# Down projection of a ConvFFN layer: eight block products against seven, with the contraction in three parts

## The chip, the core and the metric

The kernel runs on one core of a Trainium2 chip. The core has a matrix engine (TensorE, PE in the profile, with PEld for its weight loads), a vector engine (VectorE, DVE), an engine for activations (ScalarE, ACT), a general one (GpSimd, POOL) and SyncE (SP), whose queue issues most of the transfers between HBM and the on-chip memory SBUF. Matmul results land in PSUM, in banks of 512 float32 per partition. The metric is the device time of one execution in microseconds, the median of several runs; a profiled execution adds a trace of every instruction.

## The reference

One layer of an encoder, for 1024 prompt frames and 32 sample frames (T = 1056 columns together). After the mixing branches the layer computes

```
hf = RMSNorm(x)
[a | u] = hf @ W_up                     W_up (1024, 5632)
a = causal depthwise conv3(a) + b_conv
x = x + RMSNorm((gelu(a) * u) @ W_down) W_down (2816, 1024)
y = x + (p @ W_ple) * sigmoid(x @ W_ple_gate)
```

All is float32. To keep that precision, a matmul takes each operand as a high part and a low remainder in the type `fp32r`, and sums three products: high x high, high x low, low x high. Making the two parts of an operand costs a cast on ScalarE and a subtraction on VectorE (a "split").

## The kernel before

Activations lie with channels on the 128 partitions and tokens along the columns. The stages of interest are the last three.

**Up projection** (from about 1162 us on). 22 units, one for each 128-channel tile of `a` and `u` (`up_unit`). A unit already works in seven products of block sums (the scheme of Strassen and Winograd): rows are split into two halves of the contraction, columns into `a` and `u`, tokens into quarters of H = 264, two quarters making a token half (a pass `p`). A product takes 4 contraction tiles x 2 token halves x 3 matmuls of 264 columns. The operands' seven block sums lie split in SBUF pages (`ops`, placed by `where`), and the weights' seven parts are made for each unit by `unit_parts`: GpSimd adds blocks, ScalarE casts, VectorE subtracts, into a ring `wb` of eight slots. `prepare` keeps three parts ahead. Three PSUM tiles X, Y and Z (two banks each) take the products: X the first and third, Y the second, fourth and sixth, Z the fifth and seventh, so a tile is used again two products later, once VectorE or ScalarE (`after`) has read it. `ff_tail` applies convolution, gelu and the product with `u`, one unit late, and stores the tile into `act_d` in HBM.

**Down projection** (from 1617 to 1872 us). Three token groups of M3 = 352; in each, two halves of four output tiles; for each, 22 contraction tiles, accumulated in four PSUM banks without interruption. The activations of a group come from HBM in four chunks (`load_chunk`), split by ScalarE and VectorE (L2111, L2112). The weights are loaded and split anew for each group (`next_w`, L182, L184). `d_out` copies a bank out and sums squares. While groups 1 and 2 run, `x2_part` does for the group before what follows the sum of squares: scale by the row factor and the gain, add `x1`, split (L2173, L2174, L227).

**Final gate** (from 1872 us). For two halves of four output tiles and three groups, a block of 24 matmuls of 352 columns (`block`), then tanh, two vector operations (`y_out`, L2216 to L2218), and one block later the transposes into rows and the stores (`y_done`, L2230 to L2252).

What sets the order: each engine runs its own queue in order. That order isn't the text's; a scheduler builds it, taking the instruction that comes first in the text among those whose inputs it expects to be ready, and `behind(...)` puts a block behind the latest instruction traced on the named engines. Buffers of a pool are handed on when their last reader is done, and a transfer issued on SP's queue that waits holds those behind it.

## Time and profile before

| | |
|---|---|
| three runs, median | 1982.42 us (1981.69 to 1982.99) |
| profiled execution, first to last instruction | 1980.2 us |
| the rest of an execution, median less span | 2.2 us |
| TensorE busy | 1963.0 us of the span, 14239 matmuls |
| VectorE busy | 1388.1 us |
| ScalarE busy | 1003.0 us |
| GpSimd busy | 259.2 us |
| HBM read, written | 177.89 MB, 65.32 MB |

The trace has no figure of its own for what lies around the span, so the third row is the difference to the median of the runs. A row of a group reads: line, engine, operation, output and inputs, shapes, count, then busy us in all and mean ns of one, then idle time of that engine before them and what ended it. Durations of matmuls and of vector operations overlap those of their neighbours a little; starts don't.

### The profile page before, as it was taken

The numbers are of one execution on the slowest core, as the hardware profiler recorded it, in microseconds if no ns is written. First come the engines' busy times: TensorE is split into PE (matmuls) and PEld (weight loads), VectorE is DVE, ScalarE is ACT, GpSimd is POOL, SyncE is SP. The second block draws the span as 40 slices with busy tenths as digits, with TensorE's granted clock in tenths as the row PEclk, the third lists the DMA queues.
The fourth block names the chain that finished last, engine by engine and source line by source line (L and its number), as shares of the span: only waits on it lengthen the run. The fifth ranks groups of instructions, "written<-read, shape, count | busy, mean of one in ns | idle before, by whom it ended". The sixth has DMA issues, their size and how long they took to land.

```text
span 1980.2 us, 37208 instructions
## 1 busy us (share of the span) xinstructions
PE 1963.0 (99%) x14239; PEld 1948.0 (98%) x14239; DVE 1388.1 (70%) x3059; ACT 1003.0 (51%) x2188; POOL 259.2 (13%) x391
## 2 busy tenths in 40 slices
PE   8999999999999999999999999999999999999998
PEld 8999999999999999999999999999999999999998
DVE  6777776888878888553555878877777784655552
ACT  7667777666656666451225663333333344444332
POOL 2111110000000000012001133333343300000000
PEclk9999999999999999999999999999999999999999
DMA  8533431311122211486558662222222245665542
GB/s 265 151 98 103 129 112 59 129 51 55 57 77 58 58 56 58 128 256 212 179 168 277 215 222 87 76 87 66 91 71 79 84 165 186 214 198 170 161 134 79
DMA packets 255256, 253.57 MB, mean 128 GB/s; under 512 B 14133, under 2 KB 221992, under 8 KB 255077
## 3 DMA queue, kind: packets, MB, share of 16 engines
q1 hardware_dynamic: 244917, 218.43, 35.4%
q0 software_dynamic: 10080, 32.73, 5.4%
q8 instruction: 112, 1.84, 0.4%
q14 instruction: 67, 0.55, 0.1%
q10 hardware_dynamic: 80, 0.03, 0.0%
HBM read 177.89 MB, written 65.32 MB: 123 GB/s over the span
## 4 chain that ended last, share of the span: by engine, by line
PE 76%; issue 12%; DVE 5%; DMA 3%; ACT 2%; POOL 1%; SPq 0%; POOLq 0%; DVEq 0%; ACTq 0%
PE mm L203 9%; PE mm L205 9%; PE mm L204 9%; PE st L2014 7%; PE st L2012 7%; PE st L2013 7%; PE G L1114 2%; PE Y L1111 2%; PE G L1113 2%; PE Y L1114 2%; PE Y L1113 2%; PE G L1111 2%; PE Z L1111 1%; PE Z L1113 1%; PE Z L1114 1%
## 5 line engine op out<-in xcount | busy, mean ns | idle before, releaser
L2012 PE MATMUL st<-op,wt 128*128 128x264 f32 x1232 | 348.8, 283 | 2.8 <-ACT Sp L2023 1.4
L2014 PE MATMUL st<-op,wt 128*128 128x264 f32 x1232 | 349.7, 284 | 0.0
L2013 PE MATMUL st<-op,wt 128*128 128x264 f32 x1232 | 347.7, 282 | 0.0
L2012 PEld LDWEIGHTS st<-op,wt 128*128 128x128 f32 x1232 | 231.2, 188 | 4.5 <-ACT Sp L2023 2.0
L2013 PEld LDWEIGHTS st<-op,wt 128*128 128x128 f32 x1232 | 231.4, 188 | 0.0
L2014 PEld LDWEIGHTS st<-op,wt 128*128 128x128 f32 x1232 | 230.8, 187 | 0.0
L182 ACT CAST wh<-wr 128x1024 fp32r<-128x1024 f32 x125 | 131.2, 1049 | 187.7 <-PE mm L204 138.7
L184 DVE TENSOR_TENSOR wl<-wr,wh 128x1024 fp32r<-128x1024 f32 x114 | 139.6, 1225 | 111.5 <-ACT wh L182 99.6
L203 PE MATMUL mm<-ac,wh 128*128 128x352 f32 x528 | 170.6, 323 | 0.0
L1756 ACT CAST wt<-wu 128x512 fp32r<-128x512 f32 x126 | 77.7, 619 | 183.2 <-POOL ab L1998 82.2
L205 PE MATMUL mm<-ac,wl 128*128 128x352 f32 x528 | 169.7, 321 | 0.0
L204 PE MATMUL mm<-ac,wh 128*128 128x352 f32 x528 | 169.4, 321 | 0.0
L203 PE MATMUL mm<-La,wh 128*128 128x384 f32 (+1 forms) x480 | 158.2, 330 | 0.0
L204 PE MATMUL mm<-Lb,wh 128*128 128x384 f32 (+1 forms) x480 | 155.4, 324 | 0.5 <-DVE Lb L773 0.4
L205 PE MATMUL mm<-La,wl 128*128 128x384 f32 (+1 forms) x480 | 154.9, 323 | 0.1
L203 PE MATMUL mm<-Ra,wh 128*128 128x264 f32 x512 | 145.4, 284 | 0.0
L204 PE MATMUL mm<-Rb,wh 128*128 128x264 f32 x512 | 145.0, 283 | 0.0
L205 PE MATMUL mm<-Ra,wl 128*128 128x264 f32 x512 | 145.0, 283 | 0.0
L1757 DVE TENSOR_TENSOR wt<-wu,wt 128x512 fp32r<-128x512 f32 x126 | 101.1, 804 | 47.0 <-ACT wt L1756 47.0
L205 PEld LDWEIGHTS mm<-ac,wl 128*128 128x128 f32 x528 | 99.4, 188 | 0.0
L204 PEld LDWEIGHTS mm<-ac,wh 128*128 128x128 f32 x528 | 99.2, 188 | 0.0
L203 PEld LDWEIGHTS mm<-ac,wh 128*128 128x128 f32 x528 | 99.1, 188 | 0.0
(553 smaller groups left out, 5756.1 us busy)
## 6 DMA issues: line engine op xcount, KB each, us to landing
wr<-in_w_down_dram SPq DMA_DIRECT2D x66, 512.0 KB
wu<-in_w_up_dram SPq DMA_DIRECT2D x42, 512.0 KB
wu<-in_w_in_dram SPq DMA_DIRECT2D x36, 512.0 KB
ac<-act_d SPq DMA_DIRECT2D x66, 176.0 KB
act_d<-Up SPq DMA_DIRECT2D x21, 528.0 KB
wr<-in_w_in_dram SPq DMA_DIRECT2D x21, 512.0 KB
wr<-in_w_out_dram SPq DMA_DIRECT2D x16, 512.0 KB
wl<-wr POOLq DMA_DIRECT2D x11, 512.0 KB, 4.9
```

The source lines that it names most:

```text
L182: S.copy(hi[:], raw[:])
L184: V.tensor_tensor(lo[:], raw[:], hi[:].bitcast(F32), op=ALU.subtract)
L203: E.matmul(ps, wh, a, start=first and n == 0, stop=False)
L204: E.matmul(ps, wh, b, start=False, stop=False)
L205: E.matmul(ps, wl, a, start=False, stop=last and n == len(ks) - 1)
L1111: E.matmul(o, wh, x[0][k], start=first and k == 0, stop=False, skip_group_check=True)
L1113: E.matmul(o, wh, x[1][k], start=False, stop=False, skip_group_check=True)
L1114: E.matmul(o, wl, x[0][k], start=False, stop=k == 3, skip_group_check=True)
L1757: V.tensor_tensor(t[:, 1], src, t[:, 0].bitcast(F32), op=ALU.subtract)
L2012: E.matmul(o, wh, xh, start=first and k == 0, stop=False, skip_group_check=True)
L2013: E.matmul(o, wh, xl, start=False, stop=False, skip_group_check=True)
L2014: E.matmul(o, wl, xh, start=False, stop=k == 3, skip_group_check=True)
```

## The change

The down projection becomes twelve more units of the scheme that the up projection has. The contraction of 22 tiles is taken as 11 pairs; the even and the odd tile of a pair are the two rows of the block scheme, two neighbouring output tiles its two columns (four pairs `cp_` in all), and the token quarters its columns on the other side. The 11 pairs are taken in three parts of 3, 4 and 4 (`KP`), since the operand pages hold four: part by part all four column pairs run, and each unit adds its result to accumulators in SBUF (`acc_t`, and `S_` for a shared sum). In the third part the sums are completed, and the squares are summed on the way.

The operands of the products: `act_sums` makes four block sums of each pair of activation tiles on VectorE beside every second up unit and stores them (`s_d`); three operands are plain blocks of the stored activations (`a_d`, in place of `act_d`). At the last up unit, and at the last unit of parts 0 and 1, each operand page is loaded anew as its last product ends (`load_op`, on SP's queue) and split in the steps that `SPLIT_AT` names. Weights of the down units are read as 128-column tiles and go through `unit_parts`; the raw weights of every second down unit lie in the ring `wb`.

The last down unit runs its seven products for one token half and then for the other. The normalisation of the first half's tokens is placed into the second. The gate goes by token quarters of 264: quarters 0 and 1 for the first four output tiles, in steps of two contraction tiles interleaved with `x2_pair`, then the rest. The block sums change the rounding of the result, within float32; nothing of the computation is left out.

```diff
-    act_d = [dp.tile([P, T], F32, name=f"act_d{f}") for f in range(NF)]
+    a_d = dp.tile([P, NF, T], F32, name="a_d")
+    s_d = {o: dp.tile([P, NF // 2, 2, H], F32, name=f"s_d{o}") for o in (1, 3, 4, 5)}
...
+    KP = ((0, 3), (3, 4), (7, 4))
+    DU = [(pt, cp_) for pt in range(3) for cp_ in range(4)]
+    NU = NF + len(DU)
...
+            tag, bufs = ("wr", 2) if u % 2 else ("wb", 8)
+            pt, cp_ = DU[u - NF]
+            j0, n = KP[pt]
+            for c in (2 * cp_, 2 * cp_ + 1):
+                t.append(wp.tile([P, KT, P], F32, tag=tag, name=nm("wd"), bufs=bufs))
+                dma(t[-1][:, :2 * n], rows_cols(w_down, 2 * j0 * P, c * P, P, 2 * n)[0])
...
+    def act_sums(j):
+        (b11, b12), (b21, b22) = act_blocks(2 * j), act_blocks(2 * j + 1)
...
+        V.tensor_tensor(d, b11, b12, op=ALU.subtract)
+        V.tensor_tensor(e, b12, b22, op=ALU.subtract)
+        dma(s_d[4][:, j], d)
+        dma(s_d[3][:, j], e)
+        yield
+        V.tensor_tensor(d, d, b22, op=ALU.add)
+        V.tensor_tensor(e, b21, d, op=ALU.subtract)
+        dma(s_d[1][:, j], d)
+        dma(s_d[5][:, j], e)
+        yield
+
+    def load_op(pt, p, i):
...
+        dma(t[:, 1, :n].bitcast(F32), src)
+
+    def split_op(pt, p, i):
+        n = KP[pt][1]
+        hi, lo = (ops[p][i][:, a, :n] for a in range(2))
+        S.copy(hi, lo.bitcast(F32))
+        V.tensor_tensor(lo, lo.bitcast(F32), hi.bitcast(F32), op=ALU.subtract)
+
+    SPLIT_AT = {3: 0, 4: 1, 6: 2, 7: 3, 9: 4, 10: 5, 11: 6}
...
                 mults(i, t, first, ps)
+                if u == NF - 1:
+                    for p in range(2):
+                        load_op(0, p, i)
+                    split_step(0, n)
...
+                if u and u % 2 == 0 and n in (2, 5):
+                    if n == 2:
+                        sums_of.append(act_sums(u // 2 - 1))
+                    with behind(V):
+                        next(sums_of[-1])
...
+    def down_unit(u):
...
+                for k in range(ng):
+                    wh, wl = w[:, 0, k, :], w[:, 1, k, :]
+                    xh, xl = ops[p][i][:, 0, k, :], ops[p][i][:, 1, k, :]
+                    E.matmul(o, wh, xh, start=first and k == 0, stop=False, skip_group_check=True)
+                    E.matmul(o, wh, xl, start=False, stop=False, skip_group_check=True)
+                    E.matmul(o, wl, xh, start=False, stop=k == ng - 1, skip_group_check=True)
...
+        for ps in ((0,), (1,)) if split_p else ((0, 1),):
+            for n, (i, t, first) in enumerate(steps):
+                if ps[0] == 0:
+                    prepare(7 * u + n + AHEAD)
+                mults(i, t, first, ps)
+                if cp_ == 3 and not last:
+                    for p in range(2):
+                        load_op(pt + 1, p, i)
+                    split_step(pt + 1, n)
+                if cp_ == 0:
+                    split_step(pt, 7 + n)
+                after(i, ps)
+                if split_p:
+                    beside_last(ps[0], n)
...
+    def x2_pair(q, cp_):
...
+        for a in range(2):
+            k = 2 * cp_ + a
+            V.scalar_tensor_tensor(ak[:, a], ak[:, a], g_pffn[:, k:k + 1], rb2[tp_][:, h], op0=ALU.mult,
+                                   op1=ALU.mult)
+        V.tensor_tensor(ak, ak, x1s[n], op=ALU.add)
+        z_ = slice(2 * cp_, 2 * cp_ + 2)
+        S.copy(xh[q][:, z_], ak)
+        V.tensor_tensor(xl[q][:, z_], ak, xh[q][:, z_].bitcast(F32), op=ALU.subtract)
...
+    def beside_last(p, n):
...
+        if n == 1:
+            with behind(E):
+                x2_norm(0)
...
+        elif n == 4:
+            with behind(E):
+                x2_rows(0)
+            x2_pair(0, 0)
+            gate_parts(3)
+        elif n == 5:
+            x2_pair(0, 1)
...
+    for kp in gate_two(0):
+        if kp < 2:
+            x2_pair(0, kp + 2)
+        if kp == 1:
+            with behind(E):
+                x2_norm(1)
+        if kp == 2:
+            x2_pair(1, 0)
+        if kp == 3:
+            with behind(E):
+                x2_rows(1)
+            x2_pair(1, 1)
+    gate_parts(4)
+    gate_parts(5)
+    for kp in gate_two(1):
+        if kp < 2:
+            x2_pair(1, kp + 2)
+        if kp == 2:
+            gate_parts(6, where[1][2])
+            gate_parts(7, where[1][3])
...
+    for m, (q, cp_) in enumerate(((0, 2), (1, 2), (0, 3), (1, 3))):
+        gate_one(q, cp_)
+        for kp in range(2):
+            x2_pair(2 + m // 2, 2 * (m % 2) + kp)
+    for cp_ in range(4):
+        for q in (2, 3):
+            gate_one(q, cp_)
+    late_y(0)
```

More of the change, by code (lines that the diff above doesn't have):

```diff
@@ L2268, in layer_kernel, with ep_q, acc_of @@
-    for l in late:
-        y_done(*l)
+    ep = ctx.enter_context(right("ep"))
+    nrm = ep.tile([P, 4, 8], F32, name="nrm")
+    def ep_q(name):
+        return ep.tile([P, 2, H], F32, tag="q", name=nm(name), bufs=4)
+    sqd = [ep_q("sqd") for _ in range(2)]
+    acc_t = [ep.tile([P, 4, 2, H], F32, name=f"acc{i}") for i in range(3)]
+    acc_t = [acc_t[1], acc_t[2], acc_t[0]]
+    S_ = page(lq, 3, [P, 4, 2, H], "S").bitcast(F32)
+    def acc_of(cp_):
+        if cp_ == len(acc_t):
+            acc_t.append(page(lq, 2, [P, 4, 2, H], "acc3").bitcast(F32))
+        return acc_t[cp_]
```

437 lines of the change are left out of this document (268 added, 169 removed).

## The prediction

> **What bounds the kernel now.** First the page of the profile: its span, the share of each engine, the slices, the chain that ended last.
>
> ```profile
> span 1980.2 us, 37208 instructions
> PE 1963.0 (99%) x14239; PEld 1948.0 (98%) x14239; DVE 1388.1 (70%) x3059; ACT 1003.0 (51%) x2188; POOL 259.2 (13%) x391
> ...
> PE   8999999999999999999999999999999999999998
> PEclk9999999999999999999999999999999999999999
> ...
> PE 76%; issue 12%; DVE 5%; DMA 3%; ACT 2%; POOL 1%; SPq 0%; POOLq 0%; DVEq 0%; ACTq 0%
> ```
>
> TensorE is busy 99% of the span at a full granted clock, and no slice after the first falls under 0.9 until the end. So a matmul taken away is time gained, and an idle stretch of TensorE is time lost, whichever engine caused it. Next the windows by stage (columns: busy us of PE, PEld, DVE, ACT, POOL with counts, granted clock, DMA share, GB/s) and the instructions that read `ac`, the operand of the old down projection.
>
> ```profile
> 1200.00:1597.00 397.00, 396.52 (x3273) 396.26 (x3272) 307.07 (x470) 136.58 (x196) 135.94 (x97) 1.00 0.25 79
> 1300.00:1400.00 100.00, 100.00 (x828) 100.00 (x827) 76.77 (x120) 34.91 (x50) 34.23 (x26) 1.00 0.26 81
> 1616.86:1872.05 255.19, 255.19 (x1612) 255.13 (x1610) 144.16 (x200) 112.86 (x156) 0.00 (x0) 1.00 0.56 186
> ...
> L203 PE MATMUL mm<-ac,wh x528: 320/322/408, 1617.0 to 1871.6; 128*128 128x352 f32 x176
> L205 PE MATMUL mm<-ac,wl x528: 317/322/325, 1617.3 to 1871.9; 128*128 128x352 f32 x176
> ```
>
> A matmul's shown duration (322 ns) overlaps the next one's, so I use starts. The down stage starts 3 x 528 = 1584 matmuls of 352 columns in 1872.05 - 1617.0 = 255.1 us: 161.0 ns each. The up stage, already in block sums, starts 828 of 264 columns in 100 us: 120.8 ns. 161.0 x 264/352 = 120.8, so cost goes by columns, with no fixed part per matmul in sight. VectorE is 77% busy in the up stage (307.07/397) and 56% in the down stage.
>
> **The change, part by part.**
>
> *Products.* 3 token thirds x 8 output tiles x 22 contraction tiles x 3 matmuls = 1584 of 352 become 4 column pairs x 11 contraction groups x 7 products x 2 token halves x 3 = 1848 of 264. 1848 x 0.1208 = 223.2 us against 255.1: **-31.9 us**. The gate keeps its columns: 576 x 352 = 768 x 264. I go by the two rates above, which are in the ratio of the columns. The Trainium skill speaks against that ("TensorE: Matmul & The Clock Gate", section "Wait — 56ns, not 53.3ns?"): a warm matmul costs N/2.4 ns and a fixed 2.5 ns or so, which narrower ones pay oftener. An estimate from that page is 236.3 - 207.9 = 28.4 us saved, 3.5 less, with which the sum below would end at 1973.
>
> *What the rest costs is stall of TensorE.* VectorE prices follow; its instructions overlap their neighbours, so I take start to start.
>
> ```profile
> 1606.37 1.23 DVE L1957 TENSOR_TENSOR Up<-a,Up 128x1024 f32<-128x1024 f32 x1
> 1607.52 0.18 DVE L1958 TENSOR_TENSOR Up<-a,Up 128x32 f32<-128x32 f32 x1
> 1607.62 0.70 DVE L2027 TENSOR_TENSOR ab<-st,rbT 128x528 f32<-128x528 f32 x1
> 1608.24 0.88 DVE L2112 TENSOR_TENSOR ac<-ac,ac 128x704 fp32r<-128x704 f32 x1
> ...
> 1122.59 2.43 DVE L1686 TENSOR_TENSOR op<-z,op 128x1056 fp32r<-128x1056 f32 x2
> 1128.50 0.43 DVE L1660 TENSOR_TENSOR sq<-x 128x264 f32<-128x264 f32 x1
> 1128.85 0.43 DVE L1662 TENSOR_TENSOR x<-x 128x264 f32<-128x264 f32 x1
> 1886.46 1.07 DVE L2173 SCALAR_TENSOR_TENSOR acc<-acc,gvec,rb 128x352 f32<-128x352 f32 x2
> ...
> L1757 DVE TENSOR_TENSOR wt<-sa,wt 128x512 fp32r<-128x512 f32 x20 | 13.6, 680 | 0.0
> L1949 DVE SCALAR_TENSOR_TENSOR a<-ab,cvec,a 128x1058 f32<-128x1058 f32 x19 | 30.8, 1623 | 22.8 <-ACT a L1945 22.8
> L1953 DVE SCALAR_TENSOR_TENSOR a<-ab,cvec,a 128x1058 f32<-128x1058 f32 x20 | 26.3, 1316 | 0.0
> ```
>
> So 1056 columns cost 2.43 - 1.26 = 1.17 us, 1024 1.15, 528 0.62, 264 0.35; by the slope, 792 (three groups, token half) 0.90, 512 0.60, 384 0.46. The two-scalar form costs 1.24 at 1058 and 0.49 at 352, so 0.41 at 264.
>
> *Block sums beside the up stage.* `act_sums` puts four 528-column operations into every second unit of 168 x 0.1208 = 20.3 us: 4 x 0.62 = 2.5 us, VectorE from 77% to 89% there. Its four stores and the DMA share of 0.25 leave room; the sum rewritten at step 5 waits for a store issued at step 2, 8.7 us earlier. Each PSUM tile is used again two products later, so VectorE may be late by one product (2.9 us). Cost 0; 0 to 2.
>
> *Into the first down unit.* A unit of contraction part 0 lasts 126 x 0.1208 = 15.2 us. VectorE has in it the tail of channel tile 21 (two two-scalar operations 2.5, products 1.25, leftovers of `done` 1.5), its block sums 2.5, the splits of operands 3 to 6 for both token halves 8 x 0.90 = 7.2, seven weight parts 7 x 0.46 = 3.2, two reads of PSUM 1.2: 19.2 us, 4.0 more than it has. The old kernel had the same tail there, and splits too (L2112), but ahead of their need. The splits are needed by the very next products, and VectorE takes its queue in order. **+4**; below, 0, if the three weight parts made ahead cover it; above, 8, if the waits inside the tail (ScalarE's gelu, the store before a sum is rewritten) aren't filled.
>
> *From part to part.* At the last column pair of a part each of the 14 operand pages is loaded again as its product ends and split in steps 3 to 11: 14 x 1.17 = 16.4 us more on VectorE over two units. With weight parts and PSUM reads at the same prices (13.4 and 18.9 us) that makes 29.8 of 35.5 us from part 0 to 1, 35.3 of 40.6 from 1 to 2: it fits in sum, but a step with a split has 0.60 + 2.34 + 0.62 = 3.56 us of work in 2.9, lateness grows to about 3 us, and one step is what the banks allow. The loads: 14 x 541 KB = 7.6 MB, and 1.05 MB of weights before them on SP's queue. Each load waits there for its product's end, and behind the seventh stand the weights of the next unit but one, whose first part is due 11.6 us later: with those late, the casts on ScalarE and all behind them are late.
>
> ```profile
> 855.00:860.00 5.00, 5.00 (x44) 5.00 (x43) 3.78 (x10) 3.52 (x9) 0.54 (x1) 1.00 0.94 282
> 860.00:865.00 5.00, 5.00 (x44) 5.00 (x43) 3.57 (x11) 3.13 (x8) 0.05 (x1) 1.00 0.95 285
> 1606.00:1610.00 4.00, 4.00 (x36) 4.00 (x35) 3.90 (x7) 3.40 (x6) 0.00 (x0) 1.00 1.04 370
> ```
>
> The first two rows are bursts of 264-column loads (runs of 1056 bytes, as here), the third of 352-column ones. At 283 GB/s 8.6 MB take 30.5 us. From part 0 to 1 there are 28 us between the end of the first product and the split of the last operand; from 1 to 2, 32; into part 0, 28 for 6.5 MB (23 us). So about 2 us short at one place, partly covered. **+1.5** for both; 0 to 6. GpSimd's weight sums go on as in the up stage (135.94 us in 397, 34%), with room for the ten additions of squares that part 2 gives it: 0.
>
> *The start of the gate.* Every output channel is complete only in the last unit, so the normalisation, which the old kernel did beside the down stage for two thirds of the tokens, now stands wholly ahead of the gate. The last unit runs one token half after the other (7 x 12 x 0.1208 = 10.1 us each). Count from the second half: the broadcast of the row factors is queued behind its fifth product, 7.25 us, plus the transposing matmuls and ScalarE's copy: 8.0. Then a pair of channel tiles of a token quarter (`x2_pair`) costs VectorE 2 x 0.41 + 2 x 0.62 = 2.06 us, with a ScalarE cast inside that the next pair can fill. Until quarters 0 and 1 are through: eight pairs 16.5, products 5 and 6 with their squares 4 x 0.35 = 1.4, the low parts of gate weights 3, 4, 5 at 1.15 = 3.4, the second normalisation 1.5, the first two outputs 4 x 0.63 = 2.5: 25.3 us. The last step of the gate's first half then ends at 8.0 + 25.3 + 1.45 = 34.8, where TensorE alone would be at 10.1 + 96 x 0.1208 = 21.7: 13.1 us. If outputs and weights 4 and 5 (4.8 us) come after the pairs it is 8.3. **+11**; 6, if half of the pairs' work finds earlier gaps, to 16, if each pair also waits out its cast. After that 8 pairs (16.5 us) stand beside 192 matmuls (23.2 us) and are covered.
>
> *Small work and the end.*
>
> ```profile
> 1876.84 0.22 DVE L1561 TENSOR_SCALAR nv<-tr 128x2 f32<-128x2 f32 x2 [2.01 <-PE tr L1558]
> 1879.73 0.16 DVE L220 SCALAR_TENSOR_TENSOR nr<-rst,nr 128x3 f32<-128x3 f32 x1
> ...
> 1960.86 0.49 PE L2230 MATMUL tr<-ident,y 128*128 128x128 f32 x3
> 1965.06 0.49 PE L2230 MATMUL tr<-ident,y 128*128 128x128 f32 x3
> ...
> 1973.25 0.32 PE L205 MATMUL mm<-x2r,wl 128*128 128x352 f32 x1
> 1977.09 0.33 SPq L2246 DMA_DIRECT2D out_dram<-yr  x1
> 1968.70:1980.20 11.50, 5.95 (x38) 5.30 (x36) 2.67 (x9) 2.42 (x10) 0.00 (x0) 0.91 0.23 63
> ```
>
> The first two rows are one normalisation's small operations: 3.05 us with two others between. From one group of three transposes to the next is 4.20 us, 24 matmuls (3.86) and 0.34: 0.113 a transpose. There are 80 instead of 72, and 18 more column sums and broadcasts, most of them where TensorE waits anyway: **+1.5** (1 to 3). After the last matmul the old kernel needs 1980.2 - 1973.4 = 6.8 us. The new one has two output groups left there, five PSUM copies and three or four stores more on queues that took 0.3 and 0.5 us each: **+1.2** (0 to 3).
>
> *Sum:* -31.9 + 4 + 1.5 + 11 + 1.5 + 1.2 = -12.7. The profiled span becomes 1980.2 - 12.7 = 1967.5. The median of the runs, 1982.42, lies 2.2 us above that span; I put the same around the new one: **1969.7 us**.
>
> **The rivals.**
>
> 1. *The stalls are mostly filled.* VectorE was free 44% of the old down stage (144.16 of 255.19 busy), ScalarE 56%, and the scheduler lets work that is ready pass work that isn't. With 0, 0, 6, 1.5 and 1.0: -23.4, 1959. Against it: the gate's start has work that can't begin before the sum of squares.
>
> 2. *The stalls take all of it.* The upper ends 8, 5, 15 and 3 with -31.9 give -0.9: 1981.5, no change. For it: three neighbouring steps with more VectorE work than time. Against it: in the old transition VectorE was as full (3.90 of 4 us at 1606) and TensorE never waited.
>
> 3. *Slower: the operand loads are paced by DMA.* Place: the three changes of operands. Price at a rate r: 8.6 MB/r - 28, 8.6 MB/r - 32, 6.5 MB/r - 28. At 200 GB/s that is 15 + 11 + 4.5 = 30.5 in place of my 1.5: 1969.7 + 29 = 1998.7. It decides from about 220 GB/s down (11 + 7 + 1.5). For it: the old down stage moved 186 GB/s, and the runs are shorter now. Against it: that stage's DMA share was only 0.56, and bursts of this form reached 283.
>
> 4. *The clock falls at the gate's start.* The granted clock was 0.91 in the last window above, where TensorE was busy only half of the time. In my count the gate's start is like that, its longest idle stretch about 5 us (the outputs and weight splits, 4.8 us). With 0.91 there and until the pairs are through, 96 + 192 matmuls cost 288 x 0.1208 x 0.1 = 3.5 us more: 1973. Against it: in the first ten microseconds TensorE was busy 6.47 us and the clock stood at 1.00.
>
> ```profile
> 0.00:10.00 10.00, 6.47 (x28) 5.54 (x29) 1.90 (x11) 6.09 (x10) 7.22 (x20) 1.00 0.87 266
> ```
>
> The Trainium skill is harsher ("TensorE: Matmul & The Clock Gate", section "Why this matters for your kernels"): idle gaps over some 3 us drop the clock to half. By an estimate from that page the 96 matmuls cost 11.6 us more, half of it inside stalls: 1975. The row just shown doesn't bear it out.
>
> That the products don't save as counted isn't a rival I give weight: the up stage runs this very form at 120.8 ns.
>
> **How the numbers follow.** Forecast 0.45, rival 1 0.22, rival 2 0.20, rival 3 0.08, rival 4 0.05. Within 0.2% (4 us, about what a measurement of this kernel can tell from no change) is 1978.5 to 1986.4. Faster: forecast, 1 and 4, and a little of 2, less what the forecast's own upper end loses: 0.75. Same: most of rival 2, 0.14. Slower: rival 3 and the rest of 2, 0.11. The range runs from the low ends (0, 0, 6, 1, 0: 1957) to just past rival 2, 1985; rival 3 is left out. The forecast's own range is 1962 to 1977.
>
> **What would show it right or wrong.** Right: 1848 matmuls of 264 columns at 120.8 ns apart where they run; idle TensorE in three places, largest just after the last down unit, with VectorE's `acc` and `xl` operations named as what it waited for and VectorE near full; none in the up stage. Wrong: waits that name a DMA into the operand pages (rival 3), a granted clock under 1.00 there (rival 4), or a gate start with under 5 us idle (rival 1). The forecast fails if the idle time of TensorE between the up stage's end and the last matmul is under 10 or over 24 us.

## The result and the profile after

| | before | after |
|---|---|---|
| median of the runs | 1982.32 us (4 runs) | 2004.88 us (4 runs) |
| ratio, 95% interval | 1 | 1.0112 (1.0097 to 1.0126) |
| profiled execution | span 1980.2 us | span 2002.0 us, median 2.9 above it |

The changed kernel is 1.1% slower, although its down projection has 31.9 us less of products. First the page of the changed kernel: span, engines, the two rows of slices, and the chain that ended last.

```profile
span 2002.0 us, 38330 instructions
PE 1951.9 (98%) x14715; PEld 1930.4 (96%) x14715; DVE 1470.4 (73%) x3160; ACT 997.7 (50%) x2175; POOL 338.3 (17%) x449
...
PE   8999999999999999999999999999999979999998
PEclk9999999999999999999999999999999989999999
...
PE 15%; DVE 4%; issue 1%; ACT 1%; DMA 1%; POOL 0%; DVEq 0%; ACTq 0%; POOLq 0%
```

TensorE was busy 1963.0 us and is busy 1951.9 us, in a span that is 21.8 us longer. One slice now falls to 0.7, and the clock falls in the same slice: near 1640 us, where the down stage begins. The chain no longer runs through TensorE alone; it can't be followed back far. So the question is what TensorE waits for. The lines of the changed kernel that matter below:

- L2050 and L2051: cast (ScalarE) and subtraction (VectorE) of an operand's split; the tile is `dop`
- L1773 and L1774: cast and low part of a weight part; L1780 to L1787: the four weight sums of a unit, on GpSimd
- L2080 to L2082 and L2205 to L2207: products of the up and the down stage
- L2225 (VectorE), L2229 and L2231 (ScalarE): reads of PSUM in the down stage
- L1966 and L1970: the convolution's two-scalar operations; L2093: VectorE's first read of PSUM in an up unit

The next view is the list of waits, longest sums first (columns: us in total, times, longest).

```profile
PE st L2205 <- DVE acc L2225: 10.2, 7, 2.7
PE st L2205 <- ACT acc L2229: 9.5, 1, 9.5
PE st L2080 <- DVE Sp L2093: 4.6, 7, 0.7
PE st L199 <- ACT xh L2340: 3.2, 1, 3.2
...
PE st L2206 <- DVE dop L2051: 2.5, 2, 2.1
```

Left out is one wait of 2.5 us at the kernel's start, which the old trace has too. The others are all new: in the old trace TensorE has no wait over 0.3 us between 1216 us and the last product. No wait names a DMA into an operand page. The stages, with the starts of their first and last matmuls (columns: shortest, median and longest duration in ns, first and last start):

```profile
L2080 PE MATMUL st<-op,wt x1232: 279/282/422, 1161.5 to 1625.5; 128*128 128x264 f32 x176
L2205 PE MATMUL st<-dop,wt x616: 278/282/587, 1625.9 to 1882.0; 128*128 128x264 f32 x154
L2207 PE MATMUL st<-dop,wt x616: 278/283/425, 1626.1 to 1882.3; 128*128 128x264 f32 x154
```

The counts are as announced: 3 x 616 = 1848. The up stage's first product starts 0.5 us sooner than before (1162.0 there), the down stage's first at 1625.9 instead of 1617.0: the up stage is 9.4 us longer. From first to last product the down stage takes 256.4 us, where the old one took 254.9: +1.5. From there to the last product of the gate are 110.1 us instead of 101.4 (+8.7), and 9.6 instead of 6.9 behind it (+2.7). 9.4 + 1.5 + 8.7 + 2.7 - 0.5 = 21.8.

Not all of the 9.4 us lies beside the block sums. Between 1216 and 1600 us it is 7.1. Another 1.6 us come from a granted clock of 0.50 from 1167.9 to 1171.2 us, 50 us ahead of the first block sum; it stands behind two waits of 0.9 and 1.1 us that the kernel before has as well, there at a clock of 1.00. From 1600 us on, where the first operand splits run, it is 1.2 (and 0.5 are won back between 1176 and 1216).

The products did get 31.9 us shorter, so the down stage holds 33.4 us that are no products. Most of it is TensorE standing still or running slowly. The table has what lies between the starts of two matmuls beyond 120.8 ns (beyond 0.11 and 0.08 us at the small matmuls between them):

| where (us) | waits of 0.25 us and more | shorter ones, slow clock with them |
|---|---|---|
| 1625.9 to 1657, entry | 14.1 | 2.1 |
| 1698 to 1730, part 0 to 1 | 5.3 | 1.7 |
| 1780 to 1830, part 1 to 2 | 5.2 | 1.9 |
| 1830 to 1882.4, last units | 1.1 | 0.7 |
| 1882.4 to 1900, start of the gate | 4.1 | 1.6 |

From the up stage's end to the last matmul TensorE stood idle for 29.8 us (14.1 + 5.3 + 5.2 + 1.1 + 4.1), over the 24 us at which the prediction called itself failed.

**Why the waits are there.** Two things stand beside them in the trace. The first is what VectorE's instructions take. Two timelines, VectorE and then GpSimd (columns: start, us, engine, line, operation, tiles, shape, count):

```profile
1276.16 1.26 DVE L1959 COPY tails<-ab 128x2 f32<-128x2 f32 x1
1277.34 0.15 DVE L1961 COPY ab<-cach 128x2 f32<-128x2 f32 x1
1278.84 2.41 DVE L1966 SCALAR_TENSOR_TENSOR a<-ab,cvec,a 128x1058 f32<-128x1058 f32 x1 [1.34 <-ACT a L1962]
1281.17 0.69 DVE L2093 TENSOR_TENSOR Sp<-Sp,st 128x528 f32<-128x528 f32 x1
...
1694.03 1.26 DVE L2051 TENSOR_TENSOR dop<-dop 128x1056 fp32r<-128x1056 f32 x1 [2.18 <-ACT dop L2050]
1696.92 4.63 DVE L2051 TENSOR_TENSOR dop<-dop 128x1056 fp32r<-128x1056 f32 x2
```

```profile
1275.54 1.86 POOL L1780 TENSOR_TENSOR sa<-wu 128x512 f32<-128x512 f32 x1 [6.89 <-PE st L2082]
...
1278.84 1.29 POOL L1782 TENSOR_TENSOR wu<-wu,sa 128x512 f32<-128x512 f32 x1
...
1696.52 1.63 POOL L1781 TENSOR_TENSOR wd<-wd,wd 128x512 f32<-128x512 f32 x1
1698.24 2.19 POOL L1782 TENSOR_TENSOR wd<-wd,sa 128x512 f32<-128x512 f32 x1
```

A copy of two columns takes 1.26 us at 1276.16 and 0.15 at 1277.34. The first ends as a GpSimd addition ends, at 1277.40. The convolution's operation, 1.3 us alone, takes 2.41 at 1278.84, where a GpSimd addition of 1.29 us starts with it; and behind it stands L2093, the read for which TensorE waits. Two splits take 2.3 us each at 1696.92 while GpSimd adds, and one 1.26 just before. GpSimd's own additions of 512 columns take 1.29 us or up to 2.2. So it looks as if an instruction of the one engine waits out an instruction of the other. Operations with an operand in PSUM, as L2093, keep their 0.70 us.

The up stage of the kernel before shows which of the two waits:

```profile
1298.14 1.32 DVE L1953 SCALAR_TENSOR_TENSOR a<-ab,cvec,a 128x1058 f32<-128x1058 f32 x1
...
1298.22 2.38 POOL L1765 TENSOR_TENSOR wu<-wu,sa 128x512 f32<-128x512 f32 x1
```

VectorE's operation keeps its 1.32 us, and the addition that starts 0.08 us behind it takes 2.38 instead of 1.29. L1949, which starts 0.77 us behind a GpSimd addition, takes 1.64. Both hold in the same 17 of the 22 units; in the last two, with no GpSimd addition beside it, L1949 takes 1.32. So the one that starts second pays.

The Trainium skill says that of this chip ("SBUF — State Buffer", section "Who interferes with whom"): VectorE's second port pair is also GpSimd's only one, it is held for a whole instruction, and a VectorE instruction with two inputs in SBUF contends with a GpSimd instruction that reads SBUF. The rows with two inputs (the splits, the convolution's operations) agree with it. The copy of two columns has one input, so that sentence doesn't cover its 1.26 us. The prediction had not taken the sentence up.

The second thing is how lateness becomes a wait at the entry. The longest wait, followed back (PE, ScalarE, GpSimd, VectorE):

```profile
1649.01 0.59 PE L2205 MATMUL st<-dop,wt 128*128 128x264 f32 x1 [9.47 <-ACT acc L2229]
...
1647.12 1.34 ACT L1773 CAST wt<-wd 128x384 fp32r<-128x384 f32 x3 [6.75 <-POOL wd L1782]
1648.36 0.60 ACT L2229 ACTIVATE acc<-st 128x528 f32<-128x528 f32 x1
...
1643.38 3.71 POOL L1782 TENSOR_TENSOR wd<-wd,sa 128x384 f32<-128x384 f32 x1 [6.20 <-DVE wt L1774]
...
1642.66 0.55 DVE L1774 TENSOR_TENSOR wt<-wd,wt 128x384 fp32r<-128x384 f32 x1
```

TensorE waits for a PSUM read of 0.60 us on ScalarE, an engine that is half idle. The read stands in ScalarE's queue behind three casts of weights for the next unit. The casts wait for GpSimd's sum. The sum waited 6.20 us for VectorE's low part, and that stood behind the tail of channel tile 21 and the splits. A late VectorE stops TensorE here through two other queues.

### The profile page after: what moved, and what is told of

The parts are those of the page before. It is cut to its first block, busy times and chain, and to the rows that moved or that the text cites. A ratio compares the mean times of both kernels' runs of the same rounds, so it can differ in the third digit from the quotient of the medians.

```text
span 2002.0 us, 38330 instructions
## 1 busy us (share of the span) xinstructions
PE 1951.9 (98%) x14715; PEld 1930.4 (96%) x14715; DVE 1470.4 (73%) x3160; ACT 997.7 (50%) x2175; POOL 338.3 (17%) x449
## 5 line engine op out<-in xcount | busy, mean ns | idle before, releaser
L2080 PE MATMUL st<-op,wt 128*128 128x264 f32 x1232 | 350.7, 285 | 8.0 <-DVE Sp L2093 4.6
L2082 PE MATMUL st<-op,wt 128*128 128x264 f32 x1232 | 350.4, 285 | 0.0
L2080 PEld LDWEIGHTS st<-op,wt 128*128 128x128 f32 x1232 | 232.0, 188 | 11.6 <-DVE Sp L2093 6.1
L2082 PEld LDWEIGHTS st<-op,wt 128*128 128x128 f32 x1232 | 231.5, 188 | 0.0
L2205 PE MATMUL st<-dop,wt 128*128 128x264 f32 x616 | 177.5, 288 | 20.8 <-DVE acc L2225 10.2
L2206 PE MATMUL st<-dop,wt 128*128 128x264 f32 x616 | 176.4, 286 | 2.5 <-DVE dop L2051 2.5
L2207 PE MATMUL st<-dop,wt 128*128 128x264 f32 x616 | 176.6, 287 | 0.0
L1773 ACT CAST wt<-wu 128x512 fp32r<-128x512 f32 x126 | 77.0, 618 | 155.8 <-PE st L2082 65.2
L2205 PEld LDWEIGHTS st<-dop,wt 128*128 128x128 f32 x616 | 117.9, 191 | 23.2 <-ACT acc L2229 9.8
L2206 PEld LDWEIGHTS st<-dop,wt 128*128 128x128 f32 x616 | 117.9, 191 | 3.0 <-DVE dop L2051 3.0
L2207 PEld LDWEIGHTS st<-dop,wt 128*128 128x128 f32 x616 | 117.7, 191 | 0.0
L1774 DVE TENSOR_TENSOR wt<-wu,wt 128x512 fp32r<-128x512 f32 x126 | 92.6, 743 | 29.5 <-ACT wt L1773 29.5
L200 PEld LDWEIGHTS mm<-Rb,wh 128*128 128x128 f32 x512 | 96.5, 188 | 0.0
L199 PEld LDWEIGHTS mm<-Ra,wh 128*128 128x128 f32 x512 | 96.4, 188 | 0.0
```

The source lines that it names most:

```text
L199: E.matmul(ps, wh, a, start=first and n == 0, stop=False)
L200: E.matmul(ps, wh, b, start=False, stop=False)
L1773: S.copy(t[:, 0, :n], src)
L1774: V.tensor_tensor(t[:, 1, :n], src, t[:, 0, :n].bitcast(F32), op=ALU.subtract)
L2080: E.matmul(o, wh, xh, start=first and k == 0, stop=False, skip_group_check=True)
L2082: E.matmul(o, wl, xh, start=False, stop=k == 3, skip_group_check=True)
```

## The experiments

Theory A: at the operand changes VectorE has more work than time, because it and GpSimd take turns, and the queues on ScalarE pass the lateness on. Rival B: only the amount of VectorE's work counts. Rival C: the operands' DMAs are late. The clock is asked for by itself. The results, each beside runs of the kernel before on the same chip:

| run | median us | to the kernel before, us | ratio (95%) |
|---|---|---|---|
| the change | 2004.88 | +22.6 | 1.0112 (1.0097 to 1.0126) |
| e1_sums_on_vector | 1991.68 | +10.5 | 1.0046 (1.0026 to 1.0066) |
| e2_no_low_part | 1983.06 | +1.8 | 1.0007 (0.9996 to 1.0018) |
| e3_no_block_sums | 1997.26 | +16.0 | 1.0075 (1.0046 to 1.0104) |
| e4_no_weight_sums | 1985.52 | +4.3 | 1.0020 (1.0009 to 1.0031) |
| e5_sums_spread | 1988.93 | +7.4 | 1.0037 (1.0022 to 1.0053) |
| e6_two_sweeps | 2009.25 | +27.8 | 1.0139 (1.0109 to 1.0169) |
| e7_two_sweeps_gpsimd | 2010.20 | +28.7 | 1.0143 (1.0126 to 1.0160) |
| e8_late_last_sums | 1980.78 | -1.1 | 0.9997 (0.9988 to 1.0007) |
| e9_two_sweeps_spaced | 1993.89 | +12.0 | 1.0059 (1.0042 to 1.0076) |
| e10_read_first | 1977.44 | -4.4 | 0.9978 (0.9969 to 0.9987) |
| e11_clock_kept | 1974.78 | -7.1 | 0.9966 (0.9953 to 0.9978) |

### The weight sums: on VectorE, and left out

```
e1   -        adder = V if u < 1 else G
     +        adder = V if u < 1 or u >= NF else G
e4   +        if u >= NF: s1 = a21          # no sums in the down stage
     +        else: (the four additions as before)
```

> Edit: in the down stage the four weight sums of each unit run on VectorE instead of GpSimd; nothing else. GpSimd is then idle beside the operand changes. Theory A (the two engines' two-operand work takes turns, and the 9.8 us stall at the entry is a row of weight casts in ScalarE's queue that wait for GpSimd's sums): the splits of the operands take 1.25 us each instead of 1.57 in the mean, VectorE gains about 4 to 5 us per operand change from that and loses 4 x 0.65 us per unit, so that the part changes stay within 4 us of what they were; the 9.8 us stall falls under 5 us; 1996 to 2003 us. Rival B (only the amount of VectorE's work counts): VectorE has 2.6 us more per unit and is already full for 35 us at each change, the splits stay at 1.57 us, the stalls grow by 3 to 5 us at each of three changes: 2012 to 2020 us. Rival C (the operands' DMAs are late): no difference, 2002 to 2007 us.

> Edit: the four weight sums of each unit are left out in the down stage alone (the products use plain blocks, so the output is not the reference's); VectorE's list of work is unchanged, GpSimd has next to nothing. Theory A (GpSimd's additions slow VectorE's two-operand work by taking turns with it, and hold ScalarE's casts): the splits take 1.25 us, the two part changes lose 6 to 12 us of their 13, the entry's 9.8 us stall falls under 3 us with its clock fall: 1982 to 1990 us. Rival B (VectorE's own amount): VectorE's work is what it was, so only the queue effect at the entry may go; splits stay at 1.57 us, the part changes stay at 13 us: 1993 to 2005 us.

The instructions of an operand split in the changed kernel, in e1 and in e4 (there L2055): shortest, median and longest ns, first and last start.

```profile
L2051 DVE TENSOR_TENSOR dop<-dop x42: 966/1250/2352, 1613.0 to 1812.6; 128x1056 fp32r<-128x1056 f32 x28, 128x792 fp32r<-128x792 f32 x14
```

```profile
L2051 DVE TENSOR_TENSOR dop<-dop x42: 974/1252/1262, 1613.9 to 1806.1; 128x1056 fp32r<-128x1056 f32 x28, 128x792 fp32r<-128x792 f32 x14
```

```profile
L2055 DVE TENSOR_TENSOR dop<-dop x42: 976/1254/1268, 1611.7 to 1797.9; 128x1056 fp32r<-128x1056 f32 x28, 128x792 fp32r<-128x792 f32 x14
```

With GpSimd's additions gone the longest split is 1.27 us instead of 2.35. In e4 VectorE's list is what it was, and 18.3 of the 22.6 us over the kernel before are gone: rival B falls. In e1 VectorE has four additions more in each unit, and 12.1 us are gone all the same, more than theory A expected. The waits at the part changes shrink from 10.5 us to 3.6. At the entry the long wait stays, though theory A had it under 5 us: in e1 the casts wait for a sum on VectorE's own list.

```profile
1645.71 1.34 ACT L1773 CAST wt<-wd 128x384 fp32r<-128x384 f32 x3 [7.96 <-DVE wd L1782]
1646.96 0.60 ACT L2229 ACTIVATE acc<-st 128x528 f32<-128x528 f32 x1
```

At the entry 11.6 us of waits stay in e1. In e4, where nobody adds, 8.5 stay, and its longest is 4.8 us where theory A had it under 3:

```profile
1644.93 0.26 ACT L2284 COPY tl<-tr 44x128 f32<-44x128 f32 x1 [6.83 <-DMA s_d<-sm]
```

TensorE waits there for a PSUM read (L2235) that stands on ScalarE behind this copy of the convolution's last columns, and the copy waits for the stores of the last block sums. So two causes are apart: the part changes were mostly the turn-taking; the entry is a list on VectorE that is too long whoever adds, passed on by the order of ScalarE's queue.

### The splits' subtraction left out

```
e2   -        V.tensor_tensor(lo, lo.bitcast(F32), hi.bitcast(F32), op=ALU.subtract)   # in split_op
```

> Edit: the subtraction of the operands' split is left out for all three parts of the contraction (the low half keeps the whole value, so the output is not the reference's); the cast on ScalarE, every DMA and every product stay. Theory A and rival B (VectorE late at the operand changes): 42 subtractions of 0.95 to 2.3 us leave VectorE, the stalls of the entry and of both part changes vanish with their clock falls, 28 to 34 us: 1970 to 1978 us, and the up stage keeps its seven waits of 0.8 us. Rival C (DMA late): the stalls stay, 2000 to 2007 us.

20.7 us are gone, not the 28 to 34 that were expected if VectorE were all. At the entry 5.5 us of waits stay (3.7 and 1.8 us). The first is for a read behind ScalarE's own casts and operations, which pause for only 0.84 us in the ten before it. The second is for a read behind the copy of the convolution's last columns, which waits 4.91 us for the stores of the last block sums, as in e4. What stays in the middle of the down stage is this (GpSimd, ScalarE and SyncE's queue near the second part change):

```profile
1783.32 1.29 POOL L1780 TENSOR_TENSOR sa<-wd 128x512 f32<-128x512 f32 x1 [12.74 <-DMA wd<-in_w_down_dram]
...
1787.38 1.66 ACT L1773 CAST wt<-wd 128x512 fp32r<-128x512 f32 x3 [2.53 <-POOL wd L1782]
...
1764.88 6.17 SPq L2045 DMA_DIRECT2D dop<-s_d  x5
1772.15 1.82 SPq L2045 DMA_DIRECT2D dop<-a_d  x2
1774.08 2.96 SPq L1757 DMA_DIRECT2D wd<-in_w_down_dram  x2
```

The raw weights of the next unit are asked for behind the operand loads, in one queue. GpSimd's first sum waits for them, the casts wait for its third, and a PSUM read stands behind all: 2.1 us of TensorE at 1787.8. So DMA has a part, but through the weights behind the operands, and only once VectorE is out of the way. Rival C as stated (the operands late, no change by this edit) falls.

### The block sums of the up stage

e3 leaves the sums out for ten of the eleven pairs of tiles (the plain blocks are stored in their place); e5 keeps them and moves half of them, with the weight sums as in e1.

```
e3   +        if j < NF // 2 - 1: (store b11, b12, b21, b22; no additions)
e5   -                if u and u % 2 == 0 and n in (2, 5):
     +                if u > 1 and n == 2:          # first pair in the even unit, second in the odd one
```

> Edit: in the up stage the sums of blocks are left out for ten of the eleven pairs of tiles; the plain blocks are stored in their place (the output is not the reference's), so that the number and size of the stores stay. Theory (VectorE's four additions of 0.70 us in every second unit push the first PSUM read behind the next unit's product): the seven waits of 0.8 us go and the up stage is 8 to 10 us shorter, the rest stays: 1994 to 1998 us. Rival (the stores, or contention with GpSimd alone, slow the up stage): up stage shorter by under 3 us, 2001 to 2006 us.

> Edit: the down stage's weight sums on VectorE as in e1_sums_on_vector, and in the up stage the second pair of block sums moves from step 5 of the even unit to step 2 of the odd unit that follows, so that each unit holds two of VectorE's additions instead of none or four. Theory (four additions of 0.70 us in one unit push the start of the next convolution, whose 1.3 us form then stands ahead of the first PSUM read and takes 2.4 us beside GpSimd): the waits of 0.8 us go, the up stage gets 4 to 8 us shorter and the down stage is as in e1_sums_on_vector: 1984 to 1988 us. Rival (the load of VectorE as such, or its contention with GpSimd, costs the time wherever the additions stand): under 2 us are won, 1990 to 1993 us.

The same 384 us of the up stage, in the kernel before, the changed one, e3, e5 and e10 (columns: PE, PEld, DVE, ACT, POOL busy with counts, clock, DMA share, GB/s):

```profile
1216.00:1600.00 384.00, 384.00 (x3172) 384.00 (x3172) 295.44 (x456) 133.00 (x190) 131.18 (x93) 1.00 0.24 77
```

```profile
1216.00:1600.00 384.00, 378.96 (x3114) 377.29 (x3113) 319.25 (x481) 130.88 (x186) 122.20 (x94) 1.00 0.31 103
```

```profile
1216.00:1600.00 384.00, 383.51 (x3167) 383.30 (x3166) 293.80 (x447) 131.27 (x187) 132.03 (x94) 1.00 0.33 105
```

```profile
1216.00:1600.00 384.00, 381.72 (x3134) 379.83 (x3134) 300.23 (x482) 129.32 (x186) 136.66 (x94) 1.00 0.31 104
```

```profile
1216.00:1600.00 384.00, 384.00 (x3173) 384.00 (x3172) 302.33 (x492) 129.47 (x188) 132.89 (x92) 1.00 0.32 107
```

The changed kernel gets 58 matmuls fewer done in it (3172 - 3114, 7.0 us). Without the sums it is back at 3167; the stores, which e3 keeps, cost next to nothing. Its whole up stage is 6.9 us shorter than the changed kernel's, less than the 8 to 10 expected: the slow clock at 1168 us is in it too. But the sums aren't too much for VectorE: it is busy 319 of 384 us. With the second pair moved into the odd unit the seven waits of 0.8 us go; one of 0.4 us in every second unit takes their place, and e5 won 3.0 us over e1, less than expected. With that pair behind the fourth product (e10, below) the stage is as fast as before, 3173, sums and all, and VectorE's busy time falls to 302. The price was in the place: four additions in one unit push the convolution's copies and its first operation to where they stand beside GpSimd's additions and ahead of a PSUM read.

### The operand changes spread out by two sweeps

e6 orders each part as two sweeps over the column pairs, so that one sweep's operands are loaded and split during the other. e7 is e6 with GpSimd's sums; e9 spaces the operand loads.

```
e6   -    DU = [(pt, cp_) for pt in range(3) for cp_ in range(4)]
     +    B_, A_ = (1, 3, 5), (0, 2, 4, 6)
     +    DU = [(pt, s, cp_) for pt in range(3) for s in (B_, A_) for cp_ in range(4 if pt < 2 else 3)]
     +    DU.append((2, tuple(range(7)), 3))
e9   -    for p in range(2): load_op(pt + 1, p, i)          # two loads per step, at the sweep's end
     +    for a in load_at.get((u, n), ()): load_op(*a)     # one load per step or per second step
```

> Edit: as e5_sums_spread, and in the down stage the seven products of a part run as two sweeps over the four pairs of output tiles, first products 1, 3 and 5 for all pairs, then 0, 2, 4 and 6 (the last pair of the last part keeps all seven together). The operands of one sweep are then loaded and split during the other one: 6 or 8 splits over 35 to 46 us of products instead of 14 in about 30 us. The raw weights are loaded twice, and a pair needs five weight sums instead of four. Theory A (VectorE is late because the splits stand too close together): no wait over 1 us at the part changes, at most 4 us in all at the entry, gate start and tail as in e1_sums_on_vector: 1964 to 1974 us, faster than the kernel before. Rival B (the sum of VectorE's work over the down stage decides): it has 12 x 0.6 us more, no gain over e5_sums_spread: 1984 to 1992 us. Rival C (the doubled weight loads pace it: 11.5 MB more): waits on the raw weights' DMA, over 1985 us.

> Edit: as e6_two_sweeps, but the down stage's weight sums back on GpSimd. Theory A (turn-taking of the two engines costs time only where VectorE has no slack): splits and low parts slow again to 1.5 us and 0.77 us in the mean, but only the entry suffers from it, 1 to 6 us more than e6_two_sweeps: 1967 to 1980 us. Rival B (VectorE's amount of work alone decides): VectorE has 37 us less to do than in e6_two_sweeps, so this is the faster of the two by 2 us or more.

> Edit: e6_two_sweeps, with the loads of the next operands issued one at a time, one per step or per second step of the other sweep, in place of two per step in a row; the raw weights of a short unit asked for one step sooner; the last pair's block sums and the transposes as in e8_late_last_sums. Theory C (in e6_two_sweeps the raw weights stand behind eight operand loads of 528 KB in one queue, so that ScalarE and VectorE idle 10 to 14 us at 1704 to 1718 us and TensorE waits for weights): the waits in the middle of the down stage fall from 13 us to under 4 us, entry under 7 us: 1975 to 1985 us. Rival (the added weight work of the two sweeps itself is too much): waits of 1 to 2 us stay at most units: 1995 to 2008 us.

e6 is slower than what it started from. Its splits no longer come in a heap, but the raw weights are loaded twice, and they stand behind eight operand loads. VectorE, then ScalarE, after the first part's sweep:

```profile
1710.63 0.70 DVE L2270 TENSOR_TENSOR acc<-acc,st 128x528 f32<-128x528 f32 x1 [3.29 <-PE st L2252]
1714.61 0.70 DVE L2270 TENSOR_TENSOR acc<-acc,st 128x528 f32<-128x528 f32 x1 [3.27 <-PE st L2252]
...
1718.37 0.62 ACT L1778 CAST wt<-wd 128x512 fp32r<-128x512 f32 x1 [13.84 <-DVE wd L1786]
```

VectorE has nothing to do for most of 1705 to 1715 us, and ScalarE waits 13.84 us for a weight sum: rival C, in this kernel. e7, with the sums on GpSimd, is the same within its interval, so it tells nothing between A and B. e9 wins 15.7 us over e6, but it has e8's change at the entry (below) besides the spaced loads, so that not all of this is the spacing. Waits stay, five of them of 1.4 to 2.2 us, 10 us in all between 1690 and 1860, and the time lies between the two expectations. What sets those was not followed further; the sweeps were given up.

### The entry, the order of reads, and the clock

e8 takes the last pair's block sums out of the entry; e10 reads PSUM ahead of the splits; e11 gives TensorE something to do in the wait at the gate's start.

```
e8   -    for _ in act_sums(NF // 2 - 1): pass                   # right behind the up stage
     +        if u in (NF + 1, NF + 2): next(sums_of[-1])        # two additions behind each unit
e10  -                split_step(...); after(i, ps)
     +                after(i, ps); split_step(...)
     -                if u > 1 and n == 2:
     +                if u > 1 and n == 2 + u % 2:
e11  +            for _ in range(16): E.matmul(bs[0][:, 0, :H], gw[0][0][:, 0, ALL], ops[1][6][:, 0, 0, :], ...)
```

> Edit: e5_sums_spread, and the block sums of the last pair of tiles, which only the last part of the contraction reads, move from the end of the up stage to behind the second and third unit of the down stage; the transposes of the convolution's last columns go behind the third unit's products. That takes 4 x 0.62 us of VectorE out of the 33 us at the entry in which it has no idle time. Theory A (VectorE's list at the entry is longer than the time): the entry's 11 us of waits shrink by 2.5 to 4 us: 1984 to 1987 us. Rival (the wait is set by the queue on ScalarE and the weights' arrival): unchanged, 1987.5 to 1990 us.

> Edit: e8_late_last_sums, with the second pair of block sums behind the fourth instead of the third product of the odd units (each odd unit still has a wait of 0.38 us for the PSUM read that stands behind them), and in the down stage each step's PSUM read issued before the operand splits of that step instead of behind them. Theory A (what is left of the waits is VectorE's order of work): the ten waits of 0.38 us go (4 us) and the part changes' 4 us of waits halve: 1974 to 1978 us. Rival (VectorE's list is simply full, so that a read taken first makes a split late): the up stage alone gains, 1977 to 1980 us.

> Edit: e10_read_first, and 16 products of 128 x 264 on old data, into a PSUM bank that the next product clears, in the 3.4 us in which TensorE waits at the gate's start. If the granted clock falls to 0.50 because TensorE stands still for that long: the clock stays at 1.00 at the gate's start and 1.3 to 1.8 us are won over e10_read_first. If the clock falls for another reason (what the engine is given next, or the end of the stage): the fall stays, and the time is the same within 0.5 us.

The 30 us around the entry in e5 and in e8:

```profile
1616.00:1646.00 30.00, 19.33 (x135) 18.34 (x134) 29.93 (x50) 16.14 (x27) 0.00 (x0) 0.78 0.51 179
```

```profile
1616.00:1646.00 30.00, 25.74 (x194) 24.73 (x192) 28.27 (x47) 18.82 (x31) 0.00 (x0) 0.94 0.44 144
```

Four additions (2.5 us) and the transposes moved, and the waits there fall from 12.0 us to 5.2; 59 matmuls more fit in. e8 gained 8.5 us over e5, more than twice what was expected. A list that is longer than its time may cost more than its surplus, since each late result holds a queue, and waits of 3.9 and 6.4 us had also cost clock. But the order on ScalarE changed with it: in e5 the PSUM read at 1644.21 stands behind three casts of weights, in e8 it comes at 1633.72, five us ahead of them. This run doesn't part the shorter list from the better order. e10 wins 3.3 us more: the up stage is repaired, the part changes' waits fall from 4.0 to 3.7 us only, and the entry's are 6.4 again. So the reads' order was no gain in the down stage, as the rival had it.

For the clock, windows of the changed kernel at its longest wait:

```profile
1639.00:1649.00 10.00, 0.54 (x3) 0.23 (x2) 8.57 (x14) 2.97 (x6) 3.87 (x2) 0.50 0.27 108
1649.00:1653.00 4.00, 3.99 (x20) 3.99 (x21) 1.60 (x3) 0.86 (x3) 1.17 (x1) 0.56 0.22 80
1653.00:1657.00 4.00, 4.00 (x34) 3.83 (x33) 0.70 (x1) 1.20 (x2) 0.00 (x0) 1.00 0.34 99
```

and the gate's start in e10 and e11:

```profile
1858.00:1862.00 4.00, 2.08 (x9) 1.87 (x10) 3.45 (x8) 2.84 (x4) 0.00 (x0) 0.78 0.66 183
1862.00:1866.00 4.00, 4.00 (x29) 4.00 (x29) 4.00 (x9) 1.08 (x3) 0.00 (x0) 0.80 0.51 130
```

```profile
1858.00:1862.00 4.00, 2.90 (x22) 2.49 (x21) 3.94 (x10) 1.71 (x3) 0.00 (x0) 1.00 0.70 181
1862.00:1866.00 4.00, 3.91 (x32) 3.70 (x31) 3.73 (x8) 2.08 (x3) 0.00 (x0) 1.00 0.36 92
```

With 16 products on old data in the wait the clock stays at 1.00, and the first gate products run at full speed. Short gaps and slow clock from 1854 to 1870 us fall from 1.8 to 0.7 us. The traces show about 1 us won there, less than the 1.3 to 1.8 expected; the medians differ by 2.7 us, the profiled spans by 0.5, so the size of the gain isn't settled. At this place, then, the clock fell because TensorE stood still. e11 is faster than both kernels: 1974.78 us, ratio 0.9966 (0.9953 to 0.9978) to the kernel before.

## Why the prediction was wrong

The forecast was 1969.7 us; 2004.88 was measured, outside the range. Term by term, against the profiled spans:

| term | predicted us | measured us |
|---|---|---|
| products | -31.9 | -31.9 |
| block sums beside the up stage | 0 (0 to 2) | +9.4 |
| into the first down unit | +4 (0 to 8) | +16.1 |
| from part to part | +1.5 (0 to 6) | +14.0 |
| last down units | 0 | +1.8 |
| start of the gate | +11 (6 to 16) | +5.7 |
| small work | +1.5 (1 to 3) | +4.5 (what is left in the down and gate stages) |
| end | +1.2 (0 to 3) | +2.7 |

With the start 0.5 us sooner the right column makes +21.8, the difference of the spans.

- **"So cost goes by columns, with no fixed part per matmul in sight"** was right, and the 3.5 us that the Trainium skill's fixed part would have cost did not appear: 120.8 ns a start wherever the products run at a full clock.
- **"GpSimd's weight sums go on as in the up stage ... 0"** is the step that failed. The old down stage had GpSimd at 0.00 us, so every VectorE price taken from there was a price without it. With it, splits took up to 2.35 us instead of the 1.17 I used. By e1 and e4, taking those sums off GpSimd is worth 12 to 18 of the 35 us between forecast and result, the queue at the entry included. The trace of before had it in sight: among the rows of the prediction stand the two-scalar operations L1949 and L1953, same engine, same shape, 1623 and 1316 ns in the mean. I took the cheaper one as the price and did not ask why the other was dearer: it starts behind a GpSimd addition. And the row set against rival 2, VectorE at 3.90 of 4 us without a wait, has GpSimd at 0.00.
- **"Into the first down unit: +4"** priced lateness as VectorE's surplus (its terms add to 19.4 us, not 19.2, which changes little). Measured were 14.1 us of waits and 2.1 of short gaps and slow clock. What I left out is the queue: the read that TensorE needs stood on ScalarE behind casts that waited for a sum that waited for VectorE. e8 shows how steep this is: 2.5 us of work and a few transposes taken away, with the order on ScalarE that came of it, gave 8.5.
- **"It fits in sum, but ... lateness grows to about 3 us, and one step is what the banks allow"** was the right place and the right mechanism. The size was off, since the sum (29.8 of 35.5 us) had no room for GpSimd's turns: in e1 the waits there are 3.6 us, not far from the +1.5.
- **"Block sums beside the up stage ... Cost 0"** was wrong by some 7 of the 9.4 us; 1.6 of them are the slow clock ahead of the first sum, and 1.2 belong to the entry. The mean load of VectorE (77 to 89%) said that there was room, and there was: e10 has the sums at no cost. The mean says nothing of which instruction a PSUM read stands behind.
- **"The start of the gate: +11"** was too much by half. The scheduler let the pairs' work fill earlier gaps; 4.1 us of waits and 1.6 of short gaps and slow clock were left, just under the lower bound. A gate start with under 5 us idle was named as rival 1's sign, and here rival 1 was right.
- **The rivals.** Rival 3, the one slower case, had the right sign and came nearest (1998.7), by the wrong cause: in the changed kernel no wait of TensorE names the operand loads, and e2 shows a DMA at two places only, worth some 2 us each, neither of them an operand load that is late. Rival 2 had the right mechanism, VectorE late at the operand changes, and its upper ends (8 and 5 us) were still a half to a third of what came. Rival 4's clock was real. "The row just shown doesn't bear it out" was wrong, since that row was misread: it prints a clock of 1.00, but TensorE ran at half speed in it. The same transposes start 213 ns apart at 2.54 us and 109 ns apart at 12.20 us, so 12 of them take 2.82 us and then 10 take 1.32:

```profile
2.54 2.82 PE L736 MATMUL tr<-ident 128*128 128x128 f32 x12 [2.54 <-POOL ident masks.py:199]
...
12.20 1.32 PE L736 MATMUL tr<-ident 128*128 128x128 f32 x10
```

The 0.91 that the prediction took for the gate was no price either: there the clock fell at 1978.1 us, behind the last matmul. The Trainium skill's sentence ("TensorE: Matmul & The Clock Gate", section "Why this matters for your kernels": idle gaps over some 3 us drop the clock to half) agrees with the changed kernel's rows: 0.50 for some 3.5 us behind each wait of 2.7 us or more, worth 1.3 to 1.7 us each. But 3 us is no sharp bound here, on either side. In e4 a wait of 2.2 us near 1697 was followed by 0.50, and in e6 one of 2.1 at 1586; in six of the thirteen traces so were the two waits of 0.9 and 1.1 us near 1167. In e6 one of 2.45 us at 1715 was followed by 1.00, and in e1 one of 3.3 us that ended at 1637.4 was followed by two microseconds at 1.00.

What stays open: why e9 keeps its waits, what of the entry's last 5.2 us (in e8) could go, and what decides whether a wait of two to three us costs clock.

## What to carry to other kernels

Before pricing an engine's work from old rows, look at what stood beside those rows: VectorE's operations on two SBUF operands and GpSimd's additions take turns, and two means for one form in a trace can be the sign of it. Follow each PSUM read that TensorE needs through the queue it stands in, back to the slowest engine; a full engine can be paid several times over through the queues of idle ones. Extra work that fits in the mean is to be put where no read stands behind it: here the same additions cost some 7 us in one step and nothing in another. And read the clock off the distance of the matmuls' starts, not off a column alone.

## What the runs showed of the hardware

- VectorE and GpSimd took turns by whole instructions, and the one that started second paid: a GpSimd addition that started 0.08 us behind a VectorE operation took 2.38 us instead of 1.29, while that operation kept its 1.32. A copy of two columns took 1.26 us instead of 0.15, ending with a GpSimd addition; a split of 1056 columns took up to 2.35 instead of 1.25. VectorE's operations with a PSUM operand kept their 0.70 us. Four additions a unit on VectorE, mostly 0.55 to 0.70 us each, in place of four on GpSimd of 1.0 to 2.2 us (one of 3.7), were a gain of 12.1 us.
- The granted clock of the changed kernel fell to 0.50 for some 3.5 us behind waits from 2.7 us on; in other runs it fell behind waits of 2.1 us and stayed at 1.00 behind one of 3.3. 16 products on old data inside a wait of 3.4 us kept it at 1.00.
- In the first 12 us of the kernel before, transposes started 213 ns apart, and 109 ns apart from then on, while the profile's clock column printed 1.00 for both.
